# The sum over three encoder branches, made by DMAs that add instead of by GpSimd

## The chip, the core and the metric

The kernel runs on one core of a Trainium2 chip. Its metric is the device time of one execution in microseconds (us). The engines are named as in the profile: PE is the matmul engine and PEld its weight load, DVE the vector engine, ACT the scalar engine, POOL is GpSimd, SP the engine whose queue starts the transfers. SBUF is the memory on the core, PSUM the banks into which PE writes, DRAM the memory off the core.

## What is computed

Two request groups, of 256 and 512 tokens, go through the same two layers. A layer normalizes its input, projects it once, runs three mixers on the projections, and joins them:

```
def encoder_layer(x, ...):
    h = rms_norm(x, norm_g)
    proj = h @ w_in
    ...
    ya = window_attention(aq, ak, av, attn_sink) * silu(az)
    yb = mlstm_bidir(...) * sigmoid(mo) * silu(mz)
    yc = rms_norm(ssd_bidir(...) * silu(sz), ssm_norm_g)
    ga, gb, gc = split(sigmoid(gates), 3)
    merged = ga * (ya @ w_att_out) + gb * (yb @ w_mlstm_out) + gc * (yc @ w_ssm_out)
    return x + merged @ w_out
```

The change is about the two plus signs of `merged`, a matrix of 1024 channels by 768 tokens.

## The kernel before

All 768 tokens of both groups are worked on together. Channels are tiled by 128, so `merged` is eight tiles, c = 0 to 7, of 128 channels by 768 tokens in float32 (384 KB each). Every matmul operand is held as two parts, a rounded high half and the remainder as low half, and a product takes three matmuls. A piece of weights is loaded by SP into a raw slot of tile F, ACT casts its high half into tile R (`CAST R<-F`), DVE or POOL makes the low half (`TENSOR_TENSOR R<-F,R`), and this split (`split_w`) frees the raw slot, into which SP then loads the fourth piece after it.

A layer is a list of items in the order of the table `ORDER`, each a set of matmuls. The names that matter here:

- `oa0` to `oa7` (`item_O`): gate and output product of the first branch for tile c; the result is stored to a DRAM buffer `mg`.
- `ob0` to `ob7` (`item_O` with `second`): the same for the second branch. The task `put` forms gate times product on DVE (`th`), POOL adds `old`, which is the first branch's tile loaded back from `mg`, and the sum is stored to a second DRAM buffer.
- `gc`, `sz`: gates of the third branch, and its inputs. The gates stay in SBUF as tiles `g`.
- `oc0` to `oc7` (`item_P`): the product of the third branch. `put` forms gate times product in `g` on DVE, POOL adds `old`, which `fetch` has loaded from the second buffer up to five tiles ahead, ACT casts the sum to the high half of tile H (`CAST H<-F`), DVE makes the low half (`TENSOR_TENSOR H<-F,H`).
- `item_W`: the product with `w_out`, from H, for six tiles of tokens. Its first tile walks through the eight channel tiles k = 0 to 7 and so needs the sums of all eight c in turn. Its weights are eight pieces wo0 to wo7; channel tile k needs wo(2*(k//2)) and the next one. After it in the stream of pieces stand the next layer's aq0 to aq3 and akv0, akv1. In layer 0 `item_W` also starts `load_consts` for layer 1 after its first tile: two small loads, `cstb` and `cstc`, and then three scalings on POOL, behind which POOL makes the norms of the next layer.

Beside the items run the mixers, as generators on two lanes. The one that runs during `ob` is `mix_ssd`. Its `head(h)` loads two 128 by 768 tiles for each of eight heads from the DRAM buffer `csd`, makes two planes of twelve 128x128 operations and a product on DVE, and ends in matmuls of 64 columns.

The order of all instructions is fixed when the program is written: `Clock` keeps a model of when each engine is free and when each piece of memory is ready, and `tick` lets a waiting task go on when its data should be there by that model. Each engine then runs its own list in order, and so does SP's queue. A wait at the head of a list holds all that stands behind it.

Of the kernel before, what the change touches and what calls it, by code (L numbers as in the profile page):

```python
# [9 lines left out]
F32 = mybir.dt.float32  # L10
F32R = mybir.dt.float32r
AF = mybir.ActivationFunctionType
ALU = mybir.AluOpType
AX = mybir.AxisListType

NL = 2
# [16 lines left out]
TOK = 768  # L33
# [64 lines left out]
def piece_shape(piece):  # L98
    return len(piece[2]), sum(n for _, n in piece[3])


class Arena:
# [7 lines left out]
    def __init__(self, ap, words):  # L110
        self.ap, self.words = ap, words
        self.holes = [(0, words)]
# [250 lines left out]
class Watch:  # L363
    def __init__(self, nc, clock):
        self.tensor = Watched(nc.tensor, "pe", clock)
        self.vector = Watched(nc.vector, "dve", clock)
        self.scalar = Watched(nc.scalar, "act", clock)
        self.gpsimd = Watched(nc.gpsimd, "pool", clock)
        self.sync = Watched(nc.sync, "dma", clock)


class Task:
# [35 lines left out]
class Body:  # L408
    def __init__(self, tc, es, ins, outs):
        self.tc = tc  # L410
        self.ins, self.outs = ins, outs
        self.clk = Clock()
        nc = self.nc = Watch(tc.nc, self.clk)
        sb = es.enter_context(tc.tile_pool(name="sb", bufs=1))
        ps = es.enter_context(tc.tile_pool(name="ps", bufs=1, space=bass.MemoryType.PSUM))
        dr = es.enter_context(tc.tile_pool(name="dr", bufs=1, space=bass.MemoryType.DRAM))
        RW, FW, WSLOT = 12288, 20096, 2048
        self.H = sb.tile([128, 2, KD, TOK], F32R, name="H")
        rt = sb.tile([128, RW + 4 * WSLOT], F32R, name="R")
        self.R = Arena(rt[:, 0:RW], RW)  # L420
        self.wslots = [rt[:, RW + WSLOT * j:RW + WSLOT * j + WSLOT] for j in range(4)]
        ft = sb.tile([128, FW], F32, name="F")
        self.F = Arena(ft, FW)
        self.psum = ps.tile([128, 8, 512], F32, name="psum")
        for t in (self.H[:, 0, 0, :], rt[:, 0:8], ft[:, 0:8]):
            self.clk.add(t)
        self.clk.add(self.psum[:, 0, :], True)
        self.held = [False] * 8
        self.x1 = dr.tile([TOK, D], F32, name="x1")
        self.mg = [dr.tile([8, 128, TOK], F32, name=f"mg{i}") for i in range(2 * NL)]  # L430
        self.tg = [dr.tile([8, 128, TOK], F32, name=f"tg{i}") for i in range(NL)]
        self.csd = [dr.tile([2, 48, 128], F32, name=f"csd{i}") for i in range(NL)]
        self.md = [dr.tile([2, 24, 128], F32, name=f"md{i}") for i in range(NL)]

        self.K = self.F.alloc(K_N).ap
        nc.sync.dma_start(out=self.K[:, K_ID:K_ID + 128], in_=ins["kst"][:, K_ID:K_ID + 128])
        self.ident = self.K[:, K_ID:K_ID + 128]
        self.masks = (self.K[:, K_MF:K_MF + 128], self.K[:, K_MB:K_MB + 128])
        self.expo = self.F.alloc(8).ap
        nc.vector.memset(self.expo, -0.5)  # L440
        self.raw_slots = [self.F.alloc(1024).ap for _ in range(2)]
        self.raw_extra = []
        self.cb = Ring(self.F, 1, CB_N)
        self.cc = Ring(self.F, 1, CC_N)
        self.zz = self.F.alloc(224).ap
        nc.vector.memset(self.zz, 0.0)
        self.ones = self.F.alloc(1).ap
        nc.vector.memset(self.ones, 1.0)

        self.pieces = []  # L450
        self.items = []
        self.wide, self.extra = set(), set()
        off = 0
        for l in range(NL):
            for kind, name, idx, pcs in item_plan(l):
                ids = []
                for p in pcs:
                    k, c = piece_shape(p)
                    ids.append(len(self.pieces))
                    self.pieces.append((off, k, c))  # L460
                    off += 128 * k * c
                self.items.append((l, kind, name, idx, ids))

                if kind == "W":
                    self.wide.update(ids)
                if name in ("akv", "sz"):
                    self.extra.update(ids)
        self.raw_of, self.w_of, self.w_task = {}, {}, {}
        self.n_raw = self.n_split = self.asked = 0
        self.raw_drop = []  # L470
        self.tasks = []
        self.done = {}
        self.lanes = [[], []]
        self.h_task, self.h_high = {}, [False] * NT
        self.S = [dict() for _ in range(NL)]
# [736 lines left out]
    def item_O(self, l, name, c, ids):  # L1212
        nc, s = self.nc, self.S[l]
        second = name == "ob"
        if c == 0:
            self.finish_mixer((l, "M", 3) if second else (l, "A1"))
        th = self.falloc(TOK)
        old = None
        if second:
            old = self.falloc(TOK)  # L1220
            nc.sync.dma_start(out=old.ap, in_=self.mg[2 * l][c])
        w = self.weights(ids[0])
        p = self.gbank()[:, 0:TOK]
        self.mm_c(p, *w, self.hT, KD)
        nc.scalar.activation(out=th.ap, in_=p, func=AF.Tanh, scale=0.5)
        self.give(p)
        self.drop(ids[0])
        w = self.pair_weights(c, ids[1:])
        p = self.gbank()[:, 0:TOK]
        y = [s["yb", i] if second else s["ya", i] for i in range(4 if second else 2)]  # L1230
        self.mm_c(p, *w, self.y_rhs(y), 4)
        if c % 2:
            self.drop(self.pair)
        if c == 7:
            for x in y:
                x.free()

        def put():
            nc.vector.scalar_tensor_tensor(out=th.ap, in0=th.ap, scalar=1.0, in1=p, op0=ALU.add, op1=ALU.mult)
            self.give(p)  # L1240
            yield
            if second:
                nc.gpsimd.tensor_tensor(out=th.ap, in0=th.ap, in1=old.ap, op=ALU.add)
                old.free()
                yield
            nc.sync.dma_start(out=self.mg[2 * l + second][c], in_=th.ap)
            th.free()

        s["ot", name, c] = self.spawn(put())

    def fetch(self, l, c):

        s, nc = self.S[l], self.nc
        olds = s.setdefault("olds", {})
        for j in range(c, min(c + AHEAD, 8)):
            if j in olds:
                continue
            if (l, "S") not in self.done or ("gt", j) not in s or j > c and self.F.left() < RESERVE:
                break
            self.finish(s["ot", "ob", j])  # L1260
            olds[j] = self.falloc(TOK)
            nc.sync.dma_start(out=olds[j].ap, in_=self.mg[2 * l + 1][j])
            if ("gc", j) not in s:
                self.finish(s["gt", j])
                s["gc", j] = self.falloc(TOK)
                nc.sync.dma_start(out=s["gc", j].ap, in_=self.tg[l][j])

    def item_P(self, l, name, c, ids):
        nc, s = self.nc, self.S[l]
        if c == 0:  # L1270
            for i in range(NT):
                self.finish(s["szt", i])
            self.more_raw(2)
        self.fetch(l, c)
        old, g = s["olds"].pop(c), s.pop(("gc", c))
        w = self.pair_weights(c, ids)
        p = self.gbank()[:, 0:TOK]
        self.mm_c(p, *w, self.y_rhs([s["yc"]]), 4)
        if c % 2:
            self.drop(self.pair)  # L1280
        if c == 7:
            s.pop("yc").free()

        def put():
            nc.vector.scalar_tensor_tensor(out=g.ap, in0=g.ap, scalar=1.0, in1=p, op0=ALU.add, op1=ALU.mult)
            self.give(p)
            yield
            nc.gpsimd.tensor_tensor(out=g.ap, in0=g.ap, in1=old.ap, op=ALU.add)
            old.free()
            yield  # L1290
            nc.scalar.copy(self.H[:, 0, c, :], g.ap)
            yield
            nc.vector.tensor_tensor(out=self.H[:, 1, c, :], in0=g.ap, in1=self.H[:, 0, c, :].bitcast(F32), op=ALU.subtract)
            g.free()

        s["pt", c] = self.spawn(put())
# [624 lines left out]
```

## Time and profile before

| what | value |
|---|---|
| median of 3 runs | 1697.85 us (1696.43 to 1698.03) |
| the profiled execution | 1698.3 us, of which its span is 1696.5 us |
| PE busy | 1669.7 us, 98% of the span |
| DVE busy | 909.3 us, 54% |
| ACT busy | 629.3 us, 37% |
| POOL busy | 299.7 us, 18% |
| DMA, mean rate | 90 GB/s |

Times in the rows are counted from the start of the span. A row of the timeline gives the start, the time from the first to the last of merged instructions, the engine, the line (L323 is the helper that records every operation, so tiles and shapes tell instructions apart), the operation, out<-in, and the count; in square brackets stands how long the engine was idle before it and what ended that.

### The profile page before, as it was taken

To read this page: it belongs to the slowest core of one execution; us is meant where nothing else is said; L and a number is where in the kernel's file an instruction comes from. 1 tells how busy PE (TensorE), PEld (TensorE's weight loads), DVE (VectorE), ACT (ScalarE), POOL (GpSimd) and SP (SyncE) were. 2 spreads that over 40 slices of the span, in tenths; PEclk is the share of its full clock that TensorE was granted. 3 is DMA by queue.
4 is the path that set the end of the run, shared out by engine and by line. 5 is a ranking of instruction groups with operands and counts; after the bars stand their busy time and mean duration, and the time that the engine had idled before them with its cause. 6 is when DMAs were issued, how large, how long until landed. Compare 5 with 4: busy or idle time off the path is not lost.

```text
span 1696.5 us, 25376 instructions
## 1 busy us (share of the span) xinstructions
PE 1669.7 (98%) x9902; PEld 1435.2 (85%) x9902; DVE 909.3 (54%) x2112; ACT 629.3 (37%) x1377; POOL 299.7 (18%) x396
## 2 busy tenths in 40 slices
PE   7999999999999999999999999999999999999999
PEld 6888889888887888888878888898888878888887
DVE  6664446454485982246356544474455859723441
ACT  5446653232332532233224466442333344232320
POOL 4513210000002112014034132100000021301220
PEclk9999999999999999999999999999999999999999
DMA  5101122222213542245211101222121145331522
GB/s 203 63 27 38 51 76 78 87 69 64 68 63 114 190 147 91 72 144 175 78 44 63 52 26 50 88 88 78 69 72 60 63 140 174 134 109 44 174 87 75
DMA packets 47880, 152.17 MB, mean 90 GB/s; under 512 B 5616, under 2 KB 6544, under 8 KB 47760
## 3 DMA queue, kind: packets, MB, share of 16 engines
q1 hardware_dynamic: 47760, 150.55, 26.4%
q8 instruction: 78, 1.28, 0.3%
q14 instruction: 42, 0.34, 0.1%
HBM read 131.51 MB, written 19.02 MB: 89 GB/s over the span
## 4 chain that ended last, share of the span: by engine, by line
PE 87%; POOL 4%; DVE 3%; issue 3%; DMA 2%; ACT 1%; SPq 0%; POOLq 0%; ACTq 0%; DVEq 0%
PE psum L323 87%; POOL F L323 4%; DVE F L323 2%; DMA F<-csd 1%; DVE R L323 1%; DMA F<-wts_dram 1%; ACT F L323 0%; DMA F<-cstb_dram 0%; ACT R L323 0%; SPq L323 0%; ACT H L323 0%; DVE H L323 0%; POOLq L323 0%; ACTq L323 0%; DVEq L323 0%
## 5 line engine op out<-in xcount | busy, mean ns | idle before, releaser
L323 PE MATMUL psum<-H,R 128*128 128x512 f32 x4800 | 887.8, 341 | 0.0
L323 PEld LDWEIGHTS psum<-H,R 128*128 128x128 f32 x4800 | 734.1, 188 | 106.7 <-issue 6.5
L323 PE MATMUL psum<-R,H 128*128 128x512 f32 (+2 forms) x1752 | 386.2, 375 | 0.9 <-DVE F L323 0.5
L323 PEld LDWEIGHTS psum<-R,H 128*128 128x128 f32 x1752 | 306.1, 188 | 54.9 <-DVE R L323 1.4
L323 DVE TENSOR_TENSOR R<-F,R 128x1024 fp32r<-128x1024 f32 (+3 forms) x178 | 220.0, 1244 | 237.2 <-ACT R L323 235.2
L323 DVE SCALAR_TENSOR_TENSOR F<-F 128x128 f32<-128x128 f32 (+5 forms) x596 | 244.4, 456 | 76.8 <-POOL F L323 33.8
L323 POOL TENSOR_TENSOR F<-F 128x512 f32<-128x512 f32 (+9 forms) x216 | 203.3, 951 | 430.8 <-DVE F L323 255.0
L323 ACT ACTIVATE F<-F 128x128 f32<-128x128 f32 (+8 forms) x432 | 201.8, 496 | 207.2 <-DVE F L323 199.8
L323 PE MATMUL psum<-F 128*128 128x128 f32 (+5 forms) x2006 | 250.7, 288 | 22.6 <-DVE F L323 13.4
L323 PEld LDWEIGHTS psum<-F 128*128 128x128 f32 (+2 forms) x2006 | 203.0, 163 | 64.8 <-DVE F L323 22.0
L323 PE MATMUL psum<-R 128*128 128x512 f32 (+2 forms) x1344 | 250.1, 336 | 0.0
L323 ACT CAST R<-F 128x1024 fp32r<-128x1024 f32 (+3 forms) x226 | 195.1, 874 | 99.4 <-DVE F L323 58.3
L323 PEld LDWEIGHTS psum<-R 128*128 128x128 f32 x1344 | 204.4, 188 | 31.3 <-issue 3.6
L323 ACT ACTIVATE F<-psum 128x768 f32<-128x768 f32 (+2 forms) x124 | 89.0, 718 | 364.9 <-PE psum L323 329.9
L323 POOL TENSOR_SCALAR F<-F 128x256 f32<-128x256 f32 (+7 forms) x112 | 72.7, 652 | 755.0 <-ACT F L323 542.8
L323 ACT COPY F<-psum 128x256 f32<-128x256 f32 (+6 forms) x262 | 95.1, 400 | 176.6 <-PE psum L323 168.8
L323 DVE SCALAR_TENSOR_TENSOR F<-F,psum 128x768 f32<-128x768 f32 (+3 forms) x124 | 88.4, 725 | 102.8 <-ACT F L323 54.4
L323 DVE SCALAR_TENSOR_TENSOR F<-psum,F 128x128 f32<-128x128 f32 (+4 forms) x75 | 37.5, 505 | 172.8 <-PE psum L323 170.7
L323 DVE TENSOR_TENSOR F<-F 128x2 f32<-128x2 f32 (+8 forms) x316 | 86.3, 283 | 42.4 <-POOL F L323 22.7
L323 DVE TENSOR_SCALAR F<-F 128x128 f32<-128x128 f32 (+5 forms) x230 | 63.0, 302 | 41.0 <-ACT F L323 22.2
L323 DVE TENSOR_TENSOR F<-F,psum 128x129 f32<-128x129 f32 (+2 forms) x104 | 35.8, 376 | 36.4 <-ACT F L323 25.6
L323 DVE CUSTOM_DVE_ANT_0 F<-psum,F 128x256 f32<-128x256 f32 (+1 forms) x96 | 40.9, 464 | 10.4 <-PE psum L323 9.1
(24 smaller groups left out, 267.0 us busy)
## 6 DMA issues: line engine op xcount, KB each, us to landing
F<-wts_dram SPq DMA_DIRECT2D x164, 512.0 KB, 3.6
mg<-F SPq DMA_DIRECT2D x32, 384.0 KB, 2.9
F<-mg SPq DMA_DIRECT2D x32, 384.0 KB, 4.2
F<-csd SPq DMA_DIRECT2D x32, 384.0 KB, 7.0
F<-x_dram SPq DMA_DIRECT2D x12, 512.0 KB, 6.3
F<-md SPq DMA_DIRECT2D x16, 384.0 KB, 4.8
x<-F SPq DMA_DIRECT2D x6, 512.0 KB, 2.6
F<-x SPq DMA_DIRECT2D x6, 512.0 KB, 3.8
```

The source lines that it names most:

```text
L323: r = fn(*args, **kw)
```

## The change

The sum is made by transfers that add. In `ob`, the tile `th` is sent to the first branch's buffer in DRAM by a DMA that adds to what stands there; the load of `old`, POOL's addition and the second buffer go away. In `oc`, a DMA reads the sum of two branches from that buffer and adds it onto `g` in SBUF; the loads ahead of time in `fetch` and POOL's addition go away. Both kinds of DMA are started from POOL's queue (`adder`). The model `Clock` counts them as transfers, as it counts those of SP, and the tiles `old` no longer take space in F.

```
+        self.adder = Watched(nc.gpsimd, "dma", clock)
...
-        self.mg = [dr.tile([8, 128, TOK], F32, name=f"mg{i}") for i in range(2 * NL)]
+        self.mg = [dr.tile([8, 128, TOK], F32, name=f"mg{i}") for i in range(NL)]
...
-        old = None
-        if second:
-            old = self.falloc(TOK)
-            nc.sync.dma_start(out=old.ap, in_=self.mg[2 * l][c])
...
+
             if second:
-                nc.gpsimd.tensor_tensor(out=th.ap, in0=th.ap, in1=old.ap, op=ALU.add)
-                old.free()
-                yield
-            nc.sync.dma_start(out=self.mg[2 * l + second][c], in_=th.ap)
+                nc.adder.dma_start(out=self.mg[l][c], in_=th.ap, accum_op=ALU.add)
+            else:
+                nc.sync.dma_start(out=self.mg[l][c], in_=th.ap)
             th.free()
...
     def fetch(self, l, c):
-        olds = s.setdefault("olds", {})
         for j in range(c, min(c + AHEAD, 8)):
-            if j in olds:
-                continue
             if (l, "S") not in self.done or ("gt", j) not in s or j > c and self.F.left() < RESERVE:
                 break
-            self.finish(s["ot", "ob", j])
-            olds[j] = self.falloc(TOK)
-            nc.sync.dma_start(out=olds[j].ap, in_=self.mg[2 * l + 1][j])
-            if ("gc", j) not in s:
+            if ("gc", j) not in s and j >= s.get("scaled", 0):
...
         def put():
             nc.vector.scalar_tensor_tensor(out=g.ap, in0=g.ap, scalar=1.0, in1=p, op0=ALU.add, op1=ALU.mult)
             self.give(p)
-            yield
-            nc.gpsimd.tensor_tensor(out=g.ap, in0=g.ap, in1=old.ap, op=ALU.add)
-            old.free()
+            yield s["ot", "ob", c]
+            nc.adder.dma_start(out=g.ap, in_=self.mg[l][c], accum_op=ALU.add)
             yield
             nc.scalar.copy(self.H[:, 0, c, :], g.ap)
```

The change also moves instructions, at three places. The first is DVE's list in layer 0 at the first two heads of the mixer that runs beside `ob`. `SCALAR_TENSOR_TENSOR F<-F 128x128` are the planes, `TENSOR_TENSOR F<-F 128x768` ends a head's tile, `128x6x64` is the end of its matmuls. Before:

```order
L323 SCALAR_TENSOR_TENSOR F<-F,psum 128x768
L323 SCALAR_TENSOR_TENSOR F<-F 128x128 x18
L323 TENSOR_TENSOR R<-F,R 128x1024
L323 SCALAR_TENSOR_TENSOR F<-F 128x128 x12
L323 SCALAR_TENSOR_TENSOR F<-F,psum 128x768
L323 TENSOR_TENSOR R<-F,R 128x1024
L323 SCALAR_TENSOR_TENSOR F<-F 128x128 x6
L323 TENSOR_TENSOR F<-F 128x768
```

and now:

```order
L323 SCALAR_TENSOR_TENSOR F<-F,psum 128x768
L323 SCALAR_TENSOR_TENSOR F<-F 128x128 x24
L323 TENSOR_TENSOR F<-F 128x768
L323 TENSOR_TENSOR R<-F,R 128x1024
L323 SCALAR_TENSOR_TENSOR F<-F,psum 128x6x64
```

The first head is finished after 24 plane operations, where 36 stood ahead of it, and on PE its 64-column matmuls stand 60 large matmuls behind the ones of 24 products that precede all heads, where 124 stood between them.

The second place is ACT's list in layer 0 from the last `oc` tiles into `item_W`, with what each instruction waits for. `CAST H<-F` takes the sum of one c, `CAST R<-F` is the first half of the split of a piece of weights. Before:

```order
L323 CAST H<-F 128x768 [waits Pool_49] x5
L323 CAST R<-F 128x1024 [waits DMAHW4_49,PE_49]
L323 CAST H<-F 128x768 [waits Pool_49] x2
L323 CAST R<-F 128x1024 [waits DMAHW5_49,DVE_49,PE_49]
L323 CAST R<-F 128x1024 [waits DMAHW6_49,PE_49,Activation_49]
L323 CAST R<-F 128x1024 [waits DMAHW7_49]
```

and now:

```order
L323 CAST H<-F 128x768 [waits DMASW4_49]
L323 CAST R<-F 128x1024 [waits DMAHW7_49,PE_49]
L323 CAST H<-F 128x768 [waits DMASW5_49]
L323 CAST H<-F 128x768 [waits DMASW6_49]
L323 CAST R<-F 128x1024 [waits DMAHW0_49,DVE_49,PE_49]
L323 CAST R<-F 128x1024 [waits DMAHW1_49,PE_49,Activation_49]
```

The places are the same; each `CAST H<-F` waits for a transfer (`DMASW`) where it waited for POOL. The `CAST R<-F` behind the tile c = 6 are those of wo4, wo5 and so on.

The third place is SP's queue in layer 0 behind the loads of the second norm's inputs. The four loads of 128x1024 are aq0 to aq3, the 128x864 are akv0 and akv1:

```order
 L323 DMA F<-ng_dram 128x1024
 L323 DMA F<-x_dram 128x1024 x2
 L323 DMA F<-wts_dram 128x1024 x4
-L323 DMA F<-wts_dram 128x864
+L323 DMA F<-wts_dram 128x864 x2
 L323 DMA F<-cstb_dram 128x192
 L323 DMA F<-cstc_dram 128x40
 L323 DMA F<-x_dram 128x1024
-L323 DMA F<-wts_dram 128x864
 L323 DMA x_69<-F 128x1024
```

The load of akv1, which stood two places behind the small loads, now stands ahead of them.

## Rows read from the trace of the kernel before

**Rows 1.** Page, part 1: busy us, share of the span, instructions, by engine.
```profile
PE 1669.7 (98%) x9902; PEld 1435.2 (85%) x9902; DVE 909.3 (54%) x2112; ACT 629.3 (37%) x1377; POOL 299.7 (18%) x396
```

**Rows 2.** Waits of PE: us in total, times, longest us.
```profile
PE psum L323 <- DVE F L323: 13.9, 12, 5.5
PE psum L323 <- ACT F L323: 6.2, 6, 1.2
```

**Rows 3.** Timeline of PE in layer 0, at the first heads beside ob.
```profile
543.83 7.33 PE L323 MATMUL psum<-H,R 128*128 128x512 f32 x40
...
567.45 1.55 PE L323 MATMUL psum<-F 128*128 128x64 f32 x12 [1.45 <-DVE F L323]
...
570.02 1.55 PE L323 MATMUL psum<-F 128*128 128x64 f32 x12 [0.26 <-DVE F L323]
```

**Rows 4.** The same place in layer 1.
```profile
1406.73 1.55 PE L323 MATMUL psum<-F 128*128 128x64 f32 x12 [1.25 <-DVE F L323]
...
1409.30 1.55 PE L323 MATMUL psum<-F 128*128 128x64 f32 x12 [0.27 <-DVE F L323]
```

**Rows 5.** Timeline of DVE and SP at the first heads, layer 0.
```profile
544.23 4.14 SPq L323 DMA_DIRECT2D F<-csd  x6
549.30 1.66 DVE L323 SCALAR_TENSOR_TENSOR F<-F 128x128 f32<-128x128 f32 x6 [7.36 <-DMA F<-csd]
...
553.72 3.24 DVE L323 SCALAR_TENSOR_TENSOR F<-F 128x128 f32<-128x128 f32 x12 [2.75 <-DMA F<-csd]
...
566.44 0.96 DVE L323 TENSOR_TENSOR F<-F 128x768 f32<-128x768 f32 x1
```

**Rows 6.** All transfers from csd: time to landing.
```profile
DMA to landing us min/median/max: 1.6/6.3/9.7
```

**Rows 7.** Timeline of the oc items, layer 0 (765.66: c = 2; 782.91: c = 6).
```profile
765.66 0.95 DVE L323 SCALAR_TENSOR_TENSOR F<-F,psum 128x768 f32<-128x768 f32 x1 [0.55 <-PE psum L323]
...
774.14 0.95 DVE L323 SCALAR_TENSOR_TENSOR F<-F,psum 128x768 f32<-128x768 f32 x1 [2.42 <-PE psum L323]
...
777.69 0.83 ACT L323 CAST H<-F 128x768 fp32r<-128x768 f32 x1 [3.41 <-POOL F L323]
...
779.25 0.95 DVE L323 TENSOR_TENSOR H<-F,H 128x768 fp32r<-128x768 f32 x1
...
782.91 0.94 DVE L323 SCALAR_TENSOR_TENSOR F<-F,psum 128x768 f32<-128x768 f32 x1
```

**Rows 8.** Timeline of DVE: the splits of wo4 and of wo5.
```profile
788.60 2.88 DVE L323 TENSOR_TENSOR R<-F,R 128x1024 fp32r<-128x1024 f32 x1
...
791.40 1.21 DVE L323 TENSOR_TENSOR R<-F,R 128x1024 fp32r<-128x1024 f32 x1
```

**Rows 9.** Timeline of PE in item_W, layer 0, and of layer 1's first transposes.
```profile
786.66 19.23 PE L323 MATMUL psum<-R,H 128*128 128x512 f32 x84
...
806.91 1.09 PE L323 MATMUL psum<-F 128*128 128x128 f32 x8 [1.02 <-DVE F L323]
```

**Rows 10.** Chain that ended last, from wo4's split to those transposes.
```profile
791.51 3.48 DMA F<-wts_dram
795.07 1.06 ACT R L323
796.15 1.24 DVE R L323
...
797.78 5.92 DMA F<-cstb_dram
```

**Rows 11.** Timeline of PE in item_W, layer 1.
```profile
1626.63 15.62 PE L323 MATMUL psum<-R,H 128*128 128x512 f32 x68
```

**Rows 12.** Page, part 6: DMA issues, count, KB each, median us to landing.
```profile
mg<-F SPq DMA_DIRECT2D x32, 384.0 KB, 2.9
F<-mg SPq DMA_DIRECT2D x32, 384.0 KB, 4.2
```

**Rows 13.** Groups of POOL by shape: busy us, mean ns of one, idle before.
```profile
L323 POOL TENSOR_TENSOR F<-F 128x768 f32<-128x768 f32 x32 | 74.0, 2311 | 226.6 <-DVE F L323 190.2 <-DMA F<-wts_dram 20.3 <-ACT R L323 16.1
```

More of the change, by code (lines that the diff above doesn't have):

```diff
@@ L1274, in item_P @@
         self.fetch(l, c)
-        old, g = s["olds"].pop(c), s.pop(("gc", c))
+        g = s.pop(("gc", c))
+        s["scaled"] = c + 1
         w = self.pair_weights(c, ids)
```

## The prediction

> **What bounds the kernel now.** I read the page's first part: PE is busy for 1669.7 of 1696.5 us [rows 1]. No other engine is near it, so an instruction taken from POOL (18%) or a transfer taken from SP's queue is worth nothing by itself; the change counts only where it makes PE wait, or ends a wait of PE. So the second view is what PE waits for: 13.9 us for DVE and 6.2 us for ACT in all [rows 2], most of it in the first 90 us, which the change doesn't touch. Of the places that it does touch, three have a PE wait: 1.45 and 0.26 us at the first two heads beside `ob` in layer 0 [rows 3], 1.25 and 0.27 us in layer 1 [rows 4], and 1.02 us ahead of the first transposes of layer 1 [rows 9]. Together they are 4.3 us, 0.25% of the time: that is all the change can win. What it can lose is set by how much room the sums have ahead of PE, and the third view, the timeline from `oc` into `item_W`, shows that there is hardly any.
>
> **What goes and what comes.** 32 additions on POOL of 2.31 us each [rows 13], 32 loads from `mg` and 16 of the 32 stores [rows 12] go; 32 adding DMAs on POOL's queue come. The first 16 (onto DRAM, in `ob`) have nobody waiting but the sums of `oc`, some 100 us later: nothing. The other 16 stand between DVE's product and ACT's `CAST H<-F`, where POOL's addition stood, and their time to landing, L, is the number that decides. No row shows an adding DMA. The nearest rows are the load of the same 384 KB, 4.2 us, and its store, 2.9 us [rows 12]. An adding DMA has to read both sides and write one. Below: it is no slower than the load alone, 4.2. Above: it is a load and then a store, 7.1. I take the middle, 5.65, with nothing for POOL's own work on the transfer, which no row shows; two loads one after the other, 8.4, are kept for the far end. POOL's addition took 2.31.
>
> The Trainium skill prices a DMA started by GpSimd at 2.0 us and the bytes at 436 GB/s ("DMA: Bandwidth & Descriptors", section "Anatomy of one DMA — SWDGE (gpsimd) path"), and says that an add moves at half the rate of a copy since it reads two sources ("Collectives: The Full Stack", section "The bandwidth ceiling: the fold count and why AG ≠ RS ≠ AR"). An estimate from the two is 2.0 + 2 x 0.9 = 3.8 us; by it the terms of `oc` below would be near 0.3 us instead of 4.7. No row here shows either figure.
>
> **From `oc` to `item_W`.** DVE's list is such that the product of c = 6 stands behind the low half of c = 4 and a split. The walk: the product of c = 4 ends at 774.14 + 0.95 = 775.09 [rows 7]. Landing + 5.65, cast 0.83, low half 0.95 [rows 7], a split 1.21 [rows 8], the product of c = 6 0.94: it ends at 784.67, where it ended at 783.85. Landing of c = 6 + 5.65 = 790.32, cast 0.83, low half 0.95, and only then the splits of wo4 and wo5, which stand behind the two on ACT and on DVE: 2 x 1.21. (Today wo4's takes 2.88 because a POOL addition runs beside it [rows 8]; that gain is in the 1.21.) So wo5 is ready at 794.52, today at 791.40 + 1.21 = 792.61.
>
> PE runs the W matmuls from 786.66 at 19.23 / 84 = 0.229 us each [rows 9]. The low half of wo5 comes in with k = 4, as the 28th matmul: 786.66 + 27 x 0.229 = 792.84. Today's room is thus 0.2 us. After the change PE waits 794.52 - 792.84 = **1.7 us**. The pieces and sums behind it (wo6 wanted at 795.4, the low half of c = 7 at 797.2, each + 1.7) come in time, 1.21 us apart. In layer 1 the same place stands 839.97 us later with the same distances [rows 11]: 1.7 us.
>
> In layer 0 more hangs on it. The chain shows that wo4's split lets SP load aq0 at 791.51, aq0's split lets SP go on to `cstb` at 797.78, 6.27 us later, and `cstb` (5.92 us to landing) lets POOL scale and then make the norm for which PE waits till 806.91 [rows 9, 10]. With akv1 ahead of `cstb` in SP's queue the chain starts from wo5's split and goes through aq1's: 794.52 + 6.27 = 800.79, so **3.0 us** later. PE's 1.7 us of that layer lie inside it. Sum here: 3.0 + 1.7 = 4.7 us.
>
> **Heads beside `ob`.** The first loads from `csd` wait for the matmuls that end at 543.9 (the 40 after them start at 543.83 [rows 3]), so SP's queue, though emptier, can't start them sooner; those matmuls stand 4 earlier now, at 7.33 / 40 = 0.183 us each [rows 3] 0.7 us. The first load feeds DVE at 549.30, the third at 553.72 [rows 5]; now 0.7 us earlier, 553.0. Behind the third plane (1.66) DVE has the merge of the first head (six more, 1.66) and its product (0.96) [rows 5]: ready at 557.3. PE gets there 60 matmuls after 543.2: 543.2 + 60 x 0.183 = 554.2. It waits **3.1 us** where it waited 1.45 + 0.26 = 1.71 (layer 0) and 1.52 (layer 1). For the later heads I set six plane operations at 1.66 against the matmuls between; they keep up, since no POOL addition slows them, with 0.6 to 1.8 us of room. Cost: 1.4 + 1.6 = 3.0 us. Bounds: both waits vanish if the loads land some 3 us sooner with fewer transfers around them, -3.2; or the loads take the longest time in the row, 9.7 [rows 6], where the third one now lands 8.4 us after its issue (553.7, issued among the six from 544.23 [rows 5]): + 1.3 each, 5.6.
>
> **Sum.** 4.7 + 3.0 = 7.7 us, on the profiled execution's own 1698.3: 1706.0. The median of the runs is 0.45 lower, so I put the same 7.7 us on 1697.85: **1705.5 us**, 0.45% slower.
>
> **The rivals.**
> - *The adding DMA is cheap (not slower).* With L = 4.2 the product of c = 6 keeps its 783.85, wo5 is ready at 783.85 + 4.2 + 0.83 + 0.95 + 2.42 = 792.25, ahead of 792.84: no wait in W, and 792.25 + 6.27 = 798.52 makes 0.7 us at `cstb`. With the heads unchanged that is 1698.6, with my 3.0 us there 1701.6; with their waits gone 1695.4. The point from which W waits is L = 4.8. For it: stores land in 2.9. Against it: the transfer reads twice, and in the crowd of loads for the norm that SP issues just there. The skill's 3.8 us falls to this side: 1701.2 with the heads' 3.0.
> - *Faster by more than 0.2%.* It needs nearly all of the 4.3 us above. At most 1693.6; the wait of 1.02 us hangs on the chain that gets longer, so I give it little.
> - *The adding DMA becomes the bound (much slower).* From L = 5.7 on, the product of c + 2 on DVE waits for the low half of c, since L + 0.83 + 0.95 + 0.95 is then more than two `oc` items, 774.14 - 765.66 = 8.48 us [rows 7], and the delay builds from c to c + 2. With 7.1 the product of c = 4 starts at 766.61 + 7.1 + 1.78 = 775.49, c = 6 ends at 787.5, wo5 is ready at 798.8: 5.9 in layer 1 and 7.3 in layer 0, with the heads 16.2: 1714.1. With 8.4: 802.7, so 9.8 + 11.2 + 3.0 = 24.0: 1721.9.
> - *The additions aren't really off the engines*: POOL could be held while it starts a transfer, up to the 2.31 us that it was busy before. That would lengthen L in `oc` and is in its bounds; in `ob` POOL has idle time (226.6 us ahead of these 32 additions [rows 13]).
>
> **How the numbers follow.** A difference of about 0.2%, 3.4 us, is what the measurement can tell from none: 1694.5 to 1701.2. Forecast (L from about 4.7 to 7.1): 0.55. Adding DMA as bound: 0.15. Cheap, and so within 0.2%: 0.26. Faster: 0.04. Slower is the first two without the part of the forecast that the heads bring back below 1701.2, about 0.03: 0.67; same 0.29; faster 0.04. The range leaves out the fastest cases and the end at 8.4: 1697 to 1718.
>
> **What would show it.** Right: a PE wait for DVE of 1 to 3 us in the first tile of `item_W` in both layers; `CAST H<-F` released by the transfer, 5 to 7 us after the product; `cstb` issued near 801 less the start of the span, with the transposes of layer 1 near 810 plus what the heads added; a PE wait near 3 us at the first head of each layer; DVE's 128x128 operations at 1.66 us for six throughout. Wrong: casts that follow their product in under 4.8 us, no PE wait in W, or a wait at the heads that is gone. If PE waits already within `oc`, the adding DMA is the bound.

## The result, and the profile after

The changed kernel takes 1712.46 us (median, 1709.96 to 1713.55), the kernel before beside it 1697.94 us: 1.0086 times as long, 95% interval 1.0073 to 1.0098, so 14.5 us slower. The profiled execution has a span of 1710.8 us, 14.3 more than before. Page, part 1 (answers [rows 1]), and part 6 of the changed kernel (answers [rows 12]; KB each, median us from issue to landing):

```profile
PE 1676.9 (98%) x9902; PEld 1439.5 (84%) x9902; DVE 887.4 (52%) x2112; ACT 631.4 (37%) x1377; POOL 254.0 (15%) x396
...
mg<-F POOLq DMA_DIRECT2D x16, 384.0 KB, 5.0
F<-mg POOLq DMA_DIRECT2D x16, 384.0 KB, 6.4
```

POOL is relieved of 46 us and DVE of 22, and PE is *busy* 7 us longer with the same 9902 matmuls: some of them ran slower. The waits of PE (answers [rows 2]; us in total, times, longest) show a new one, for ACT's casts into R:

```profile
PE psum L323 <- DVE F L323: 12.4, 9, 5.5
PE psum L323 <- ACT R L323: 7.3, 3, 3.7
```

Where the 14.3 us came from, by landmarks that have the same number of matmuls ahead of them in both lists of PE:

| stretch, up to | before | after | added |
|---|---|---|---|
| third batch of first transposes | 28.25 | 29.66 | +1.4 |
| first matmul of W, layer 0 | 786.66 | 784.76 | -3.3 |
| second batch of layer 1's transposes | 816.03 | 824.02 | +9.9 |
| first matmul of W, layer 1 | 1626.63 | 1633.27 | -1.3 |
| last 24 matmuls | 1690.06 | 1704.35 | +7.6 |

The kernel won where the prediction saw a loss (`ob`), and lost in W and right behind it nearly four times the 4.7 us that it saw there. The timeline of the changed kernel from the last `oc` items into W of layer 0 (start, us, engine; answers [rows 7 to 9]; the product of c = 4 starts at 772.24, those of c = 5 and c = 6 are the two `SCALAR_TENSOR_TENSOR`):

```profile
777.65 0.95 DVE L323 SCALAR_TENSOR_TENSOR F<-F,psum 128x768 f32<-128x768 f32 x1
777.91 0.84 ACT L323 CAST H<-F 128x768 fp32r<-128x768 f32 x1 [1.18 <-DMA F<-mg]
...
780.88 0.95 DVE L323 SCALAR_TENSOR_TENSOR F<-F,psum 128x768 f32<-128x768 f32 x1
780.99 0.33 SPq L323 DMA_DIRECT2D F<-wts_dram  x1
781.37 0.49 SPq L323 DMA_DIRECT2D F<-ng_dram  x1
781.96 0.94 SPq L323 DMA_DIRECT2D F<-x_dram  x2
782.12 0.87 POOL L323 DMA_DIRECT2D F<-mg  x1 [2.36 <-DVE F L323]
783.38 0.84 ACT L323 CAST H<-F 128x768 fp32r<-128x768 f32 x1 [3.67 <-DMA F<-mg]
...
792.01 0.83 ACT L323 CAST H<-F 128x768 fp32r<-128x768 f32 x1 [7.80 <-DMA F<-mg]
...
793.82 4.63 DVE L323 TENSOR_TENSOR R<-F,R 128x1024 fp32r<-128x1024 f32 x4
```

From the end of a product to its cast, c = 4 takes 777.91 - 773.19 = 4.7 us and c = 5 takes 783.38 - 778.60 = 4.8; c = 3 takes 4.8 too (5.1, 4.8 and 5.1 in layer 1). But c = 6 takes 792.01 - 781.83 = **10.2 us**. Four loads of 512 KB were issued within 2 us of it: wts, ng and two of x. In layer 1 it is 1640.75 - 1631.30 = 9.45 us, beside three loads. (c = 0, with loads of weights beside it, takes 9.4 us in layer 0, but has room.) The queues from 783 to 787 us, behind the issue of c = 6, show what it waits for (packets, MB, share of 16 engines; q1 carries what SP starts, q0 the adding DMAs):

```profile
q1 hardware_dynamic: 313, 1.16, 92.1%
q0 software_dynamic: 2, 0.00, 0.1%
```

For these 4 us next to nothing of the adding DMA moved, since SP's loads had the engines; only from 787 to 792 us did q0 get a share, 61.4%. PE after that, in layer 0:

```profile
784.76 5.61 PE L323 MATMUL psum<-R,H 128*128 128x512 f32 x24
793.84 0.79 PE L323 MATMUL psum<-R,H 128*128 128x512 f32 x1 [3.48 <-ACT R L323]
794.79 1.22 PE L323 MATMUL psum<-R,H 128*128 128x512 f32 x2 [0.15 <-ACT R L323]
796.24 13.69 PE L323 MATMUL psum<-R,H 128*128 128x512 f32 x53 [0.23 <-DVE R L323]
812.37 1.51 PE L323 MATMUL psum<-F 128*128 128x128 f32 x8 [2.45 <-DVE F L323]
```

and in layer 1:

```profile
1633.27 5.61 PE L323 MATMUL psum<-R,H 128*128 128x512 f32 x24
1642.58 0.80 PE L323 MATMUL psum<-R,H 128*128 128x512 f32 x1 [3.69 <-ACT R L323]
1643.52 1.22 PE L323 MATMUL psum<-R,H 128*128 128x512 f32 x2
1644.97 58.85 PE L323 MATMUL psum<-R,H 128*128 128x512 f32 x261 [0.23 <-DVE R L323]
```

The wait is not the whole of it: one matmul takes 0.8 us there, and the 53 behind 796.24 take 0.258 us each, against 0.229 before [rows 9]. The granted clock tells why. Windows of layer 1 (stretch, length, then busy us of PE, PEld, DVE, ACT, POOL; the number behind POOL's is the granted clock, 0.50 being 1.2 GHz):

```profile
1639.00:1642.00 3.00, 0.00 (x0) 0.00 (x0) 0.39 (x1) 1.25 (x2) 0.00 (x0) 1.00 0.82 159
1642.00:1644.00 2.00, 1.27 (x2) 0.74 (x3) 2.00 (x3) 2.00 (x3) 0.00 (x0) 0.59 0.00 0
...
1646.00:1648.00 2.00, 2.00 (x6) 1.61 (x5) 2.00 (x3) 0.10 (x1) 0.00 (x0) 0.50 0.00 0
1648.00:1650.00 2.00, 2.00 (x8) 1.54 (x7) 0.06 (x1) 0.00 (x0) 0.00 (x0) 0.71 0.00 0
```

From about 1642.4 to 1649.2 PE runs at 1.2 GHz. The same happens in layer 0 behind the 3.48 us, and once more behind the 2.45 us ahead of the first transposes (0.65 in 812 to 815, 0.78 in 815 to 818). In the kernel before these places stand at 1.00.

The heads beside `ob` went the other way. Timeline of layer 0 in the changed kernel (answers [rows 3, 5]):

```profile
540.74 4.58 SPq L323 DMA_DIRECT2D F<-csd  x6
...
546.85 4.86 DVE L323 SCALAR_TENSOR_TENSOR F<-F 128x128 f32<-128x128 f32 x18 [3.55 <-DMA F<-csd]
...
554.99 1.45 PE L323 MATMUL psum<-F 128*128 128x64 f32 x12
```

The loads from csd start 3.5 us earlier than before and PE has no wait there; in layer 1 one of 1.03 us is left.

### The profile page after: what moved, and what is told of

It reads as the page before. It is cut to its first block, busy times and chain, and to the rows that moved or that the text cites. A ratio compares the mean times of both kernels' runs of the same rounds, so it can differ in the third digit from the quotient of the medians.

```text
span 1710.8 us, 25333 instructions
## 1 busy us (share of the span) xinstructions
PE 1676.9 (98%) x9902; PEld 1439.5 (84%) x9902; DVE 887.4 (52%) x2112; ACT 631.4 (37%) x1377; POOL 254.0 (15%) x396
## 4 chain that ended last, share of the span: by engine, by line
PE 84%; issue 6%; POOL 4%; DMA 3%; DVE 2%; ACT 1%; SPq 0%; POOLq 0%; ACTq 0%; DVEq 0%
PE psum L323 84%; POOL F L323 4%; DMA F<-mg 2%; DVE F L323 1%; DMA F<-wts_dram 1%; DVE R L323 1%; ACT R L323 1%; ACT F L323 1%; DMA F<-cstb_dram 0%; ACT H L323 0%; DVE H L323 0%; SPq L323 0%; POOLq L323 0%; ACTq L323 0%; DVEq L323 0%
## 5 line engine op out<-in xcount | busy, mean ns | idle before, releaser
L323 PE MATMUL psum<-R,H 128*128 128x512 f32 (+2 forms) x1752 | 395.5, 381 | 8.9 <-ACT R L323 7.3
L323 PEld LDWEIGHTS psum<-R,H 128*128 128x128 f32 x1752 | 311.2, 191 | 67.2 <-ACT R L323 9.3
L323 DVE TENSOR_TENSOR R<-F,R 128x1024 fp32r<-128x1024 f32 (+3 forms) x178 | 215.4, 1218 | 254.5 <-ACT R L323 252.4
L323 DVE SCALAR_TENSOR_TENSOR F<-F 128x128 f32<-128x128 f32 (+5 forms) x596 | 228.0, 431 | 66.7 <-POOL F L323 34.8
L323 POOL TENSOR_TENSOR F<-F 128x512 f32<-128x512 f32 (+8 forms) x184 | 129.4, 714 | 205.4 <-ACT F L323 123.6
```

Of the source, the lines that this page charges most:

```text
L323: r = fn(*args, **kw)
```

## Experiments

The theory after reading the traces: the half of the change in `ob` is a gain, since SP's queue loses a store that held the loads from csd; all of the loss comes from `oc`, where the adding DMA of c = 6 meets the loads for W, PE waits, and the wait itself lowers the clock.

**Each half alone.** `e1_ob` has the adding DMA only in `ob`, `e2_oc` only in `oc`.

```
e1_ob:  -  nc.gpsimd.tensor_tensor(out=th.ap, in0=th.ap, in1=old.ap, op=ALU.add)
        +  nc.adder.dma_start(out=self.mg[l][c], in_=th.ap, accum_op=ALU.add)
e2_oc:  -  nc.gpsimd.tensor_tensor(out=g.ap, in0=g.ap, in1=old.ap, op=ALU.add)
        +  nc.adder.dma_start(out=g.ap, in_=self.mg[2 * l + 1][c], accum_op=ALU.add)
```

> Half of the change: only the sum in `ob` is made by the adding DMA (onto the buffer in DRAM); `oc` loads the stored sum ahead and POOL adds it, as before. Theory: the whole loss of 14.5 us comes from `oc`, and the half in `ob` is a gain, since SP's loads from csd no longer stand behind a store that waits for POOL's addition. Then the PE waits at the first two heads (1.71 and 1.52 us) fall to at most 1 us per layer, the W matmuls of both layers run without a PE wait over 0.3 us and with a granted clock of 1.00, and the time is 1694 to 1698 us. Rival: the DMAs onto DRAM also cost (they hold POOL or crowd the loads of weights); then PE waits appear in `ob` and the time is over 1700 us. Of the 1.4 us that the changed kernel lost between 15 and 30 us, where its granted clock was 0.80 and not 0.90: if it belongs to the execution and not to the change, this run may show either figure.

> The other half: only the sum in `oc` is made by the adding DMA (the stored sum onto the tile in SBUF); `ob` adds on POOL and stores, as before. Theory: the loss is all here. The transfer of c = 6 takes 8 to 10 us to its cast, PE waits 3 to 4 us in the first tile of W in both layers, the granted clock falls to half behind each of the two waits, and the heads wait as before (3.2 us in all, against 1.0 in the changed kernel): 1712.5 + 2.2 = 1714.7 us, in a range of 1711 to 1718. Rival: the loss needs both halves (with both, two tiles' worth of memory is free and the loads for W start earlier); then the loads for W start as late as before, the transfer of c = 6 takes under 6 us and the time is 1698 to 1704 us.

Measured: `e1_ob` 1693.02 us, ratio 0.9957 (0.9942 to 0.9972); `e2_oc` 1714.23 us, ratio 1.0084 (1.0068 to 1.0100). The gain and the loss part as the theory says, and the rival of `e2_oc` (that the loss needs both) falls: its c = 6 takes 794.35 - 783.78 = 10.6 us and PE waits 4.16 and 4.14 us, with granted clocks of 0.87 and 0.86 in the stretches of W. In `e1_ob` W runs without a wait, and the gain is even 1 us more than I had expected. Not as expected: the heads of `e2_oc` waited 1.9 us in all, not 3.2, and the halves don't add up, since -5.5 and +15.7 us make 10.1, not 14.5. From layer 1's transposes to its W the gain is 3.9 us in `e1_ob` and only 1.3 in the changed kernel; no run shows why. PE of `e1_ob`, W of layer 0 and the transposes behind it:

```profile
785.35 19.24 PE L323 MATMUL psum<-R,H 128*128 128x512 f32 x84
805.49 1.09 PE L323 MATMUL psum<-F 128*128 128x128 f32 x8 [0.89 <-DVE F L323]
```

**The crowd around c = 6.** `e3_late` is the whole change with the loads of ng and x started by ACT behind the cast of c = 7.

```
-        load(0)
...
+                    if k == 7:
+                        load(0, nc.aload)
+                        if not last:
+                            nc.aload.dma_start(out=gb.ap, in_=self.ins["ng"][...])
+                        load(1, nc.aload)
```

> The changed kernel with one thing moved: the loads of ng and of the first two tiles of x (three of 512 KB in layer 0, two in layer 1) are issued from ACT's queue behind the cast of c = 7, where SP issued them within 1 us of the adding DMA of c = 6. Theory: the 10.2 us of c = 6 are the 4.7 us of a quiet transfer plus its share of the three loads. Then its cast starts 4.6 to 5.5 us after the end of its product in both layers, PE's wait of 3.5 and 3.7 us in W falls under 0.5 us, the granted clock stays at 1.00 there, and the time is 1712.5 - 2 x 7 = about 1698 us (1695 to 1702; in layer 0 the norm now gets x later, which may cost 1 to 3 us of it). Rival: the long transfer lies in itself, in the adding onto SBUF while DVE and ACT work on it; then c = 6 takes 8 us or more again and the time stays at 1709 to 1714 us.

Measured: 1699.22 us, ratio 1.0006 (0.9993 to 1.0019). The timeline of its layer 0:

```profile
780.44 0.95 DVE L323 SCALAR_TENSOR_TENSOR F<-F,psum 128x768 f32<-128x768 f32 x1
...
788.21 0.84 ACT L323 CAST H<-F 128x768 fp32r<-128x768 f32 x1 [4.37 <-DMA F<-mg]
...
790.99 0.81 PE L323 MATMUL psum<-R,H 128*128 128x512 f32 x2 [0.44 <-ACT R L323]
...
792.44 15.98 PE L323 MATMUL psum<-R,H 128*128 128x512 f32 x69 [0.64 <-DVE R L323]
...
797.35 0.40 ACTq L323 DMA_DIRECT2D F<-x_dram  x1
```

c = 6 now takes 788.21 - 781.39 = 6.8 us (6.6 in layer 1). Three loads fewer took 3.4 us off the 10.2, so the crowd is shown as the cause of most of it; from 783 to 787 us the adding DMAs now have 54.8% of the engines, where they had 0.1%. It is not the 4.7 I expected: a load of weights and the adding DMA of c = 5 are still under way beside it. PE's waits fall to 0.64 us at most in W and the clock there stays at 1.00; 13 of the 14.5 us are back. What remains is 1.9 and 1.7 us in the two W, and in layer 0 a wait of 2.51 us ahead of the transposes: `cstb` lands at 807.63 there, among the loads that were moved, and the transposes start 3.3 us behind it (3.2 in the kernel before and in the changed one).

**Is it the wait that lowers the clock, or the adding DMAs?** Two kernels without any adding DMA: before, with ACT held ahead of the cast of c = 6 by copies of the tile onto itself.

```
+            if c == 6:
+                for _ in range((2, 5)[l]):      # e5_hold10: (5, 10)
+                    self.tc.nc.scalar.copy(g.ap, g.ap)
             nc.scalar.copy(self.H[:, 0, c, :], g.ap)
```

> The kernel before, with no adding DMA, but ACT held ahead of the cast of c = 6 by copies of that tile onto itself, unknown to the planner: two copies in layer 0 (about 1.7 us), five in layer 1 (about 4.1 us). It makes the PE wait in W by itself. Theory: a PE wait of some 3.5 us lowers the granted clock behind it to half for some 6 us, whatever it waits for. Then layer 1 shows a PE wait of 3.5 to 4 us, a granted clock near 0.5 behind it, and its W comes out 7 to 8 us later; in layer 0 the wait is 1 to 1.7 us, with no fall of the clock, and the norm is 1.7 us later: in all about 1697.9 + 3 + 7.5 = 1708 us (1705 to 1711). Rival: the clock falls for another reason that the adding DMAs bring (their traffic, or POOL's starts); then layer 1 loses its wait alone, the clock stays at 1.00, and the time is about 1705 us or less (1702 to 1705).

> Again the kernel before, without any adding DMA, with ACT held longer ahead of the cast of c = 6: five copies in layer 0 (4.3 us), ten in layer 1 (8.6 us). With two and five copies PE's wait came out at nothing and at 1.4 us, since the cast has some 1.5 us of room there; from these, five copies make 2 to 2.5 us of loss in layer 0, in several short waits, and ten make one wait of 4.5 to 5.5 us in layer 1. Theory: the half clock follows from the long wait itself. Then layer 1 shows a granted clock near 0.5 for some 6 us behind its wait and loses 8 to 9 us; layer 0 keeps 1.00 in W (its waits are under 1 us each), unless its norm then waits 2 us or more. In all 1698 + 2.5 + 2 + 8.5 = 1711 us (1707 to 1715). Rival: the clock falls only beside adding DMAs; then the clock stays at 1.00 in layer 1, which loses 5 to 6 us, and the time is 1704 to 1708 us.

Measured: `e4_hold` 1701.49 us, ratio 1.0016 (1.0003 to 1.0029). It settled nothing, as the hold was too short: no wait in W of layer 0, and three short ones (0.36, 0.45, 0.63 us) in layer 1 with the clock at 1.00. `e5_hold10` came to 1708.95 us, ratio 1.0061 (1.0048 to 1.0074), with one long wait in layer 1. Its timeline there, and the windows around:

```profile
1626.58 8.63 ACT L1293 COPY F<-F 128x768 f32<-128x768 f32 x10 [3.69 <-POOL F L323]
...
1637.07 0.80 PE L323 MATMUL psum<-R,H 128*128 128x512 f32 x1 [4.67 <-ACT R L323]
```

```profile
1630.00:1636.00 6.00, 2.40 (x11) 1.66 (x9) 0.00 (x0) 5.78 (x9) 0.00 (x0) 1.00 0.09 36
1636.00:1638.00 2.00, 0.80 (x1) 0.29 (x1) 1.90 (x2) 2.00 (x4) 0.00 (x0) 0.62 0.00 0
1638.00:1640.00 2.00, 1.76 (x3) 1.07 (x4) 2.00 (x3) 2.00 (x3) 0.00 (x0) 0.50 0.00 0
...
1644.00:1646.00 2.00, 2.00 (x11) 1.64 (x10) 0.00 (x0) 0.00 (x0) 0.00 (x0) 1.00 0.00 0
```

The fall to 1.2 GHz is there with no adding DMA in the program and next to no transfer under way; the rival falls.

**Why the heads gained.** `e6_store` is the kernel before with the store of the sum in `ob` started by POOL; it still adds on POOL, and the lists of DVE and PE are unchanged.

```
-            nc.sync.dma_start(out=self.mg[2 * l + second][c], in_=th.ap)
+            q = nc.adder if second else nc.sync
+            q.dma_start(out=self.mg[2 * l + second][c], in_=th.ap)
```

> The kernel before with one thing moved: the store of the sum in `ob` is started from POOL's queue, right behind POOL's addition, and no longer from SP's. It adds nothing; the loads of `old` and POOL's additions stay, and the lists of PE, DVE and ACT are those of before. Theory: the gain at the heads comes from SP's queue, where the six loads from csd stood behind a store that waited for POOL's addition. Then they are issued near 540.5 and not at 544.2, the 1.45 and 0.26 us of PE wait in layer 0 and the 1.25 and 0.27 us in layer 1 shrink to under 0.5 us each, and the time is 1694 to 1697 us. Rival one, as the prediction had it: the loads wait for matmuls of that place; then they are issued at 543.5 or later, and the time stays within 1 us of before. Rival two: the gain comes from POOL's additions, which slow DVE's operations beside them; then the loads are early, but the planes of the second head stay late and at least 1 us of each wait stays.

Measured: 1694.17 us, ratio 0.9975 (0.9965 to 0.9984). Its timeline at the first heads:

```profile
539.74 5.88 SPq L323 DMA_DIRECT2D F<-csd  x6
...
546.81 1.67 DVE L323 SCALAR_TENSOR_TENSOR F<-F 128x128 f32<-128x128 f32 x6 [4.52 <-DMA F<-csd]
...
566.20 1.45 PE L323 MATMUL psum<-F 128*128 128x64 f32 x12
```

All four PE waits are gone. With POOL's additions still beside DVE, the second rival falls, and so does the prediction's claim that these loads wait for matmuls. One store moved to another queue gives most of what the half in `ob` gives.

**Versions that might beat both.** `b1_ob_consts` is `e1_ob` with the small loads moved ahead; `b2_early` is the whole change with the small loads and the crowd moved ahead.

```
b1, b2:  +        if c == 2 and l + 1 < NL:
         +            self.load_consts(l + 1)
b2:      +        if c == 1:      # in item_P: the loads of x0, x1 and ng
```

> The half of the change in `ob` alone, and the small loads for layer 1 (cstb, cstc and their three scalings on POOL) moved from behind the first tile of W to the item oc2. Theory: the wait of 0.89 us ahead of layer 1's first transposes goes, since cstb is on the chip 40 us earlier, and nothing else moves: 1693.0 - 0.9 = 1692.1 us (1691 to 1693). Rival: POOL, held by the scalings ahead of its addition for c = 2, delays the sums of `oc`; they have over 10 us of room up to c = 5, so I expect no more than 0.3 us from it; 1694 us or more would speak for it.

> The whole change, with what crowds c = 6 moved ahead: the loads of ng and of the first two tiles of x are issued at oc1, and cstb and cstc at oc2. Theory: the adding DMA of c = 6 then has at most one load of weights beside it and takes 4.7 to 6.8 us to its cast; PE loses 0 to 1.9 us per layer in W, in waits too short for the clock to fall, the norm does not wait, and the gain at the heads stays: 1692 to 1697 us, so that the whole change is a gain once its transfers are alone. Rival: the crowd only moves, the sums of c = 1 to 3 come late and DVE's list carries that on to c = 6; then PE waits over 2 us in W and the time is over 1700 us.

Measured: `b1_ob_consts` 1692.11 us, ratio 0.9963 (0.9950 to 0.9976), the fastest median here; the wait ahead of the transposes is gone in its trace, but by the intervals it can't be told from `e1_ob`. `b2_early` came to 1705.67 us, ratio 1.0042 (1.0027 to 1.0056): the rival was right. Its timeline in `oc`:

```profile
774.95 0.83 POOL L323 TENSOR_SCALAR F<-F 128x64 f32<-128x64 f32 x3 [8.39 <-DMA F<-cstb_dram]
775.74 0.91 POOL L323 DMA_DIRECT2D F<-mg  x1
...
783.27 4.51 PE L323 MATMUL psum<-R 128*128 128x512 f32 x24 [1.35 <-DVE F L323]
...
795.11 0.51 PE L323 MATMUL psum<-R,H 128*128 128x512 f32 x1 [1.88 <-ACT R L323]
```

`cstb` got into the crowd that I had moved, POOL waited 8.39 us for it, and the adding DMA of c = 3 stood behind that on POOL's queue, issued 6.1 us after its product ended (769.64). DVE's list carried it on: PE waits within `oc` already. Layer 1 has no `cstb` to load, and there too the product of c = 6 came late, 1.0 us ahead of W (2.8 before), and PE waited 2.04 us.

**Only the last two tiles undone.** `e7_six` has the adding DMA for c = 0 to 5, and the load ahead and POOL's addition for c = 6 and 7.

```
+            if old is None:
                 nc.adder.dma_start(out=g.ap, in_=self.mg[l][c], accum_op=ALU.add)
+            else:
+                nc.gpsimd.tensor_tensor(out=g.ap, in0=g.ap, in1=old.ap, op=ALU.add)
```

> The whole change, but in `oc` only the tiles c = 0 to 5 get their sum by the adding DMA; for c = 6 and 7 the stored sum is loaded at oc3 and oc4 and POOL adds it, as before. Theory: the change's loss hangs on the last two tiles alone; for the others 4.7 to 10 us to the cast are covered, since W wants them later. Then PE has no wait over 0.3 us in W in either layer, the granted clock there is 1.00, the gain at the heads stays, and the time is 1692 to 1696 us, as with `ob` alone (1693.0). Rival: the slow sums of c = 0 to 5 also push DVE's list, so that the product of c = 6 comes late whatever adds to it; then 1 us of wait or more is left in W of each layer, and the time is 1697 us or more.

Measured: 1699.20 us, ratio 1.0004 (0.9990 to 1.0017). The rival was right here too. Timeline of layer 0:

```profile
782.45 0.95 DVE L323 SCALAR_TENSOR_TENSOR F<-F,psum 128x768 f32<-128x768 f32 x1
...
784.39 1.79 ACT L323 CAST H<-F 128x768 fp32r<-128x768 f32 x2 [3.12 <-DMA F<-mg]
```

The product of c = 6 ends 0.9 us before W's first matmul (784.33); in the changed kernel it was 2.9 us before. ACT's list holds the cast of c = 6 behind that of c = 5, which still waits for its DMA, and takes both in a row. PE's waits in W were 0.43 and 0.63 us, much the same in layer 1, and 2.17 us ahead of the transposes. So in every form that I tried the half in `oc` costs at least 6 us against `e1_ob`.

## Why the prediction was right or wrong

**Slower, within the range: right**, but its likeliest time (1705.5) lay 7 us low, and its terms were off in both directions. By the landmarks W and the norm behind it cost 17.5 us where the sum had 4.7, and the stretches with the heads gave back 4.6 where the sum had a cost of 3.0. That the time still fell into the range is partly luck.

**The time to landing, L: mis-sized.** I took 5.65 for all tiles, with bounds of 4.2 and 7.1 and a far end of 8.4. A tile with little traffic beside it took 4.7 to 5.1, below what I took; c = 6, on which the sum rests, took 10.2 and 9.45, beyond the far end. The failing step is that I used one L, and named the crowd "of loads for the norm that SP issues just there" only as an argument against a rival, without adding it to the price of c = 6; with three of the loads gone it took 6.8 (`e3_late`). The Trainium skill states that DMAs started by different engines run on the same 16 DMA engines and interleave ("DMA: Bandwidth & Descriptors", section "Issuing engines are not separate DMA queues"). The trace agrees from 787 us on, where both queues were served (61.4% and 44.2%), but not before: from 783 to 787 us the adding DMA had 0.1%. The estimate of 3.8 us, from the two pages named in the prediction, is below every quiet tile here.

**The walk from c = 6 to PE: right.** With L as measured it gives the end of wo5's split as 781.83 + 10.2 + 0.83 + 0.95 + 2.42 = 796.2; PE goes on at 796.24. PE wants it 27 x 0.229 = 6.18 us after W's first matmul. The same walk holds in every kernel of the table: what PE loses at this place is how late the cast of c = 6 starts after W's first matmul, less 1.95 us (the 6.18 less 4.23 from the cast to the end of wo5's split).

| kernel, layer | cast after W's start | less 1.95 | lost up to the matmul with wo5 | longest wait | lowest granted clock behind it |
|---|---|---|---|---|---|
| `e4_hold`, 0 | 1.53 | none | none | none | 1.00 |
| `e3_late`, 1 | 3.63 | 1.68 | 1.69 | 0.64 | 1.00 |
| `e3_late`, 0 | 3.86 | 1.91 | 1.91 | 0.64 | 1.00 |
| `e5_hold10`, 0 | 4.13 | 2.18 | 2.18 | 0.64 | 1.00 |
| `e4_hold`, 1 | 4.14 | 2.19 | 2.19 | 0.63 | 1.00 |
| `b2_early`, 0 | 5.66 | 3.71 | 3.70 | 1.88 | 0.50 |
| `b2_early`, 1 | 5.82 | 3.87 | 3.87 | 2.04 | 0.50 |
| changed, 0 | 7.25 | 5.30 | 5.30 | 3.48 | 0.50 |
| changed, 1 | 7.48 | 5.53 | 5.52 | 3.69 | 0.50 |
| `e2_oc`, 1 | 7.92 | 5.97 | 5.97 | 4.14 | 0.50 |
| `e2_oc`, 0 | 7.94 | 5.99 | 5.98 | 4.16 | 0.50 |
| `e5_hold10`, 1 | 8.45 | 6.50 | 6.49 | 4.67 | 0.50 |

It doesn't hold in `e7_six`: there PE lost 1.44 us in each W although the cast starts 1.03 and 0.82 us after W; POOL adds there, and in layer 0 the split of wo4 takes DVE 2.88 us beside it, where the walk has 1.21.

So the term of 1.7 us per layer became 5.3 and 5.5: 10.8 where the sum had 3.4.

**The chain over `cstb`: right in kind.** wo5's split + 6.27 gives 802.5 for its issue; it was 804.00, and the transposes waited 2.45 us. Of the 9.9 us that layer 0 lost from W's start to the second batch of transposes, 5.3 were lost at wo5 and 1.4 are the longer wait for the norm; the other 3.2 are matmuls that ran slower.

**The clock: missing.** No term of the sum was for what a wait does to the matmuls behind it. In layer 1, W lost 7.6 us, of which 5.5 at wo5: 2.1 are matmuls at the lower clock. With the 3.2 of layer 0, behind its two falls, that is 5.3 us. The Trainium skill has the pattern ("TensorE: Matmul & The Clock Gate", section "HAM oscillation — how this bites in real kernels"): a kernel whose waits for transfers let PE's clock fall starts each burst at the low level. The trace agrees: the granted clock is 0.50 behind waits of 3.5 to 4.2 us for the adding DMA, and behind 4.7 us for the held ACT.

**Heads beside `ob`: wrong in sign.** I predicted +3.0 us and kept -3.2 as a bound. The step that failed is "The first loads from `csd` wait for the matmuls that end at 543.9": two things happened at the same moment and I took one for the cause of the other. In SP's queue the store `mg<-F` stood directly ahead of the six loads, issued at 543.86, and it waited for POOL's addition. In the kernel before:

```profile
542.02 1.81 POOL L323 TENSOR_TENSOR F<-F 128x768 f32<-128x768 f32 x1 [9.40 <-DVE F L323]
...
543.86 0.33 SPq L323 DMA_DIRECT2D mg<-F  x1
```

With the store off that queue, and nothing else changed, the loads start at 539.74 (`e6_store`), so the matmuls that end at 543.9 don't hold them. With the landmarks the gain is 3.3 us up to W of layer 0 in the changed kernel, more than the 1.7 us of waits; the rest are matmuls that ran up to 2% quicker (48 in 8.48 us against 8.64), and why is open. Part of it can belong to the execution: `e4_hold` and `e5_hold10`, whose program is that of before up to there, differ from it by +0.6 and -0.8 us in this stretch. The waits vary too: the four make 3.2 us in the kernel before, and 1.8 to 1.9 in `e2_oc`, `e4_hold` and `e5_hold10`, which store from SP's queue as well. And the 4.3 us that the prediction took as the most to be won were too few: `e1_ob` won 5.5.

**The rivals.** The cheap DMA was right for quiet tiles (4.7 to 5.1 us, about its point of 4.8) and wrong where it counted. The adding DMA as the bound gave 1714.1, near the time, but its mechanism isn't what happened in layer 0 of the changed kernel: there the product of c = 6 ends 2.9 us ahead of W, as before (2.8). In layer 1 it ends 2.0 ahead, so 0.8 us of PE's loss there may be of this kind. It does show in `b2_early` and, as a late product, in `e7_six`. POOL is held 0.87 us per adding DMA, not 2.31.

**Probably not of the change: +1.4 us at the start.** The granted clock in 15 to 30 us was 0.80 in the changed kernel's profile, 0.90 before, and 0.80 to 0.91 in the nine experiments, whose programs differ little there. It varies from execution to execution; no experiment was made on it.

## What to carry to other kernels

A transfer put in the place of an engine's addition has no fixed price: cost it by what is in the DMA engines at that moment, at the one place where the consumer has least room. Before naming what a queue waits for, read which instruction stands directly ahead in it: here moving one store off SP's queue was worth 4 us by itself, and the half of the change that has no waiter is worth keeping (1693 us). A wait of PE of some microseconds costs more than its length, since the matmuls behind it start at the lower clock.

## What the runs showed of the hardware

- An adding DMA keeps the DMA engines about 1.9 times as long per byte as a plain load. The queues in 1590 to 1660 us of the changed kernel (packets, MB, share of 16 engines; q0 are the eight adding DMAs, q1 SP's):

```profile
q1 hardware_dynamic: 1872, 6.29, 27.7%
q0 software_dynamic: 1152, 3.15, 26.4%
```

  26.4 / 3.15 against 27.7 / 6.29. Where each had the engines to itself it is 1.8 times (0.78 MB at 89.8% of 773 to 778 us, against 1.16 MB at 92.1% of 783 to 787). The Trainium skill states for the adding step of a ring of cores, which reads two sources, half the rate of the copying step ("Collectives: The Full Stack", section "The bandwidth ceiling: the fold count and why AG ≠ RS ≠ AR"); the trace of this adding DMA is near that.
- PE's granted clock fell to 0.50 behind each of the long waits in the table, with adding DMAs in the program and without (`e5_hold10`); in layer 1 of the changed kernel it stayed there from 1642.4 to 1649.2. It also fell behind 2.45 us ahead of the transposes (2.51 in `e3_late`, 2.17 in `e7_six`), and in `b2_early` behind 1.88 and 2.04 us with two short waits right after. It did not fall behind the 1.45 us of [rows 3], behind 1.65 us ahead of the transposes in `e2_oc`, nor behind the three short waits in a row of `e4_hold`.
- Onto DRAM the same transfer took 5.0 us (median) beside the loads of `ob`, and a plain store started by POOL 3.1 us in `e6_store`.
